# Conditioning products in four column groups, and the context down projection and half of the block product's operands kept in the up pass, in a two-layer DiT block

## The chip, the cores and the metric

One Trainium2 chip, one core. The metric is the device time of one launch in microseconds; three runs of the kernel before gave 3122.32, 3124.87 and 3125.19, median 3124.87. Times below are of one profiled execution of the same program. Engines: TensorE (PE, its weight loads PEld), VectorE (DVE), ScalarE (ACT), GpSimd (POOL) and SyncE (SP), the last two here mostly issuing DMAs.

## The reference

Two layers over a latent of 1024 tokens and a context of 256, width 1024, all fp32. Each layer: a mixer (three token mixers, not touched here), then a gated feed-forward. Conditioning vectors `c`, `c_ctx` give per layer six modulation vectors of 1024:

```
mod   = silu(c)     @ ada_w[layer] + ada_b[layer]      # 1024 -> 6144
mod_c = silu(c_ctx) @ ada_w[layer] + ada_b[layer]
def conv_ffn(h, w_up, conv_w, conv_b, w_down):
    u = dwconv(h @ w_up, conv_w, 1) + conv_b           # 1024 -> 2 x 2816
    gate, val = split(u, 2)
    return (silu(gate) * val) @ w_down                 # 2816 -> 1024
x     = x     + g2  * conv_ffn(modulate(x, ...), ...)
h_ctx = h_ctx + g2c * conv_ffn(modulate(h_ctx, ...), ...)   # layer 0 only
```

## The kernel before, in words

The program is written with symbolic tiles; a scheduler then lays out each engine's instructions in one fixed order and adds the semaphores. It goes by the order of the source, and moves an instruction ahead where its own model of the chip holds it ready. Slots of four tags serve nearly all of SBUF: `L` ("h4", 36 slots of 128x1024), `H2` ("h2", 8 of 128x512), `X` ("h1", 12 of 128x256) and the weight tiles `wh`, `wl` (two each) and `wr`, `wd` (one each). In PSUM tag "a" has two tiles of two banks (`ps`), tag "b" four of one bank (`pb1`).

fp32 products are made of three products of rounded operands: `split` (L313 to 316) writes a rounded copy (ScalarE, L315) and the rest (VectorE, L316), and each product is high x high, high x low, low x high.

**Conditioning**, `ada_gen` (L183 to 214): for each layer and each of three parts of 2048 columns 16 steps. A step loads 128 rows by 1024 columns of `ada_w` (tile `aw`), and multiplies them with `cl`, 32 columns of which two are the conditioning vectors (L199). With only 32 columns a product fills a quarter of the array's columns; `tile_position` names the quarter, and the output stands in the same 32 partitions of PSUM. In step i the two halves of 512 columns go to the quarters 2(i % 2) and 2(i % 2) + 1. The generator is stepped from other code: at the start, in the mixers, and with `ada_load` and `ada_mm` once in each call of `up`.

**Up pass**, `ffn_up` (L1189 to 1247): for f = 0 to 21 and for gate and value (`up`) 48 products of 512 columns into `pu` (latent, two banks), in layer 0 24 of 256 columns into `puc` (context), then the three-tap convolution on ScalarE (L1225) and VectorE (L1226, 1227), Silu on the gate, and gate times value (L1236). The latent's result goes to DRAM in four quarters `actp`, by half of f (11 each) and half of the tokens; the context's stays in `actc`.

**Context down projection**, `ctx_down` (L1250 to 1270), layer 0 only: behind the pass, 22 row blocks of `w_down` (`dr`) are loaded, split, and multiplied into eight blocks of `pd` that stay open over all of f; 528 products of 256 columns, and eight additions into `xc`.

**Block product**, `lat_down` (L1272 to 1432): the latent's product with `w_down` as a two-by-two block product with seven products in place of eight (Winograd's form). Each of the seven stages goes over six `PAIRS` of row blocks, makes the weight operand A from `raw` tiles and the activation operand B from `b` tiles (L1290 loads them back from `actp`), splits both and does 24 products of 512 columns per pair; stages with `isy` = 0 add into `px`, the others into `py`. `finish` adds a stage's result into the residual (L1401), and `fins` holds the steps of the next norm or of the last norm, one of which is done behind each pair from the third on.

Of the kernel before, what the change touches and what calls it, by code (L numbers as in the profile page):

```python
# [9 lines left out]
F32 = mybir.dt.float32  # L10
# [8 lines left out]
P = 128  # L19
D = 1024  # L20
KT = 8
# [66 lines left out]
def tile_dit(ctx: ExitStack, tc: tile.TileContext, x, c, ctxt, c_ctx, ada_w, ada_b, norm_mix_g, norm_ffn_g,  # L88
# [94 lines left out]
    def ada_gen(l, t, al, order=None):  # L183
# [23 lines left out]
        for q4 in range(4):  # L207
            PE.transpose(out=pt[:, q4 * P:(q4 + 1) * P], in_=ev[:, q4 * P:(q4 + 1) * P], identity=ident)
        src = pt.rearrange("p (q j r) -> p j q r", q=4, j=4)[:, :, :, 0:2]
        b = rows["ada_b"][:, l * 48 + t * 16:l * 48 + t * 16 + 16]  # L210
        m_ = mod[l][:, t * 16:(t + 1) * 16, :].rearrange("p (j q) s -> p j q s", j=4)
        V.tensor_tensor(out=m_, in0=src,
                        in1=b.rearrange("p (j q) -> p j q", j=4).unsqueeze(3).to_broadcast([P, 4, 4, 2]), op=add)
# [930 lines left out]
    def project_out(l, y, xl, xc):  # L1144
# [18 lines left out]
        for part in range(2):  # L1163
            for m in range(KT):
# [17 lines left out]

    FH = NF // 2
    PAIRS = [(2 * j, 2) for j in range(FH // 2)] + [(FH - 1, 1)]

    actp = [[[[dp.tile([P, n, 512], F32, name=f"act{l}{a}{b}{j}") for j, (_, n) in enumerate(PAIRS)] for b in range(2)]
             for a in range(2)] for l in range(DEPTH)]

    def ffn_up(l, h, hc_, last=False):  # L1189

        WU = ffn_w_up[l]
        u_, actc = {}, []
# [6 lines left out]
        yield "ready"  # L1199

        def up(f, val):
# [7 lines left out]
            for s_, hh, n in jobs:  # L1209
# [3 lines left out]
                if s_:  # L1213
                    if val:
                        u = H2("uc")[:, 0:C]
                    else:
                        if f % 4 == 0:
                            actc.append(L("actc"))
                        u = actc[-1][:, (f % 4) * C:(f % 4 + 1) * C]
                        u_[1, f] = u  # L1220
                else:
                    u = L("u")
                    if not val:
                        u_[0, f] = u
# [3 lines left out]
                if not val:  # L1228
                    with sact if last and f == NF - 1 else ExitStack():
                        S.activation(out=u, in_=u, func=AF.Silu)  # L1230
                        if last and f == NF - 1:
                            S.preload_act_table_set(LN_EXP)
                else:
                    g = u_.pop((s_, f))
                    o = g if s_ else u
# [320 lines left out]
```

## Time and profile before

| what | value |
|---|---|
| runs, median | 3124.87 us |
| profiled execution, its own time | 3125.18 us |
| its span, first to last instruction | 3123.4 us |
| PE, DVE, ACT, POOL busy | 2971.0, 1742.1, 1313.2, 168.4 us |
| mean granted TensorE clock | 0.98 |
| moved by DMA | 329.93 MB |

The span is what the views of the trace cover; the time of a run is 1.8 us longer. An engine's busy time is no limit by itself: only the chain of waits tells which engine the end waited for. A row of a timeline names the engine, the line, the operation, what it writes and reads, how many are merged in it, and in brackets how long its engine had been idle and what ended that.

### The profile page before, as it was taken

The page shows a single profiled execution, that of the slowest core. Times are in us where ns is not written, and L with a number is a line of the kernel's source. Part 1 is how long each engine was busy: PE and PEld are TensorE (multiplying, and loading weights), DVE is VectorE, ACT ScalarE, POOL GpSimd, SP SyncE. Part 2 cuts the span into 40 slices and gives each one's busy share as a digit, 9 for nine tenths or more (in the row PEclk, how much of TensorE's full clock was granted, in tenths as well). Part 3 has the DMA queues.
Part 4 walks back from the last instruction along what each step waited for, and adds up shares of the span by engine and source line. Part 5 has one row for each costly group of instructions (what it writes and reads, how often), then busy time and mean ns, then how long its engine had stood idle before and what let it go on. Part 6 is the DMA issues. An engine that isn't in the chain of part 4 may idle for free.

```text
span 3123.4 us, 40811 instructions
## 1 busy us (share of the span) xinstructions
PE 2971.0 (95%) x16088; PEld 2325.1 (74%) x16088; DVE 1742.1 (56%) x2639; ACT 1313.2 (42%) x2219; POOL 168.4 (5%) x265
## 2 busy tenths in 40 slices
PE   6999898999999999999899899998999999999998
PEld 4867565558888888888877687776678888887776
DVE  5466555665633333334677656767746333334885
ACT  5365663673422222223334445785744222223333
POOL 1000002000000000000000000002000000000000
PEclk8999899999999999999999899999999999999998
DMA  7212146414222232113864310024044222223842
GB/s 288 67 49 61 54 133 166 135 56 149 93 88 88 86 97 88 48 61 119 285 200 145 96 29 21 25 71 106 10 154 144 72 76 68 75 74 122 295 148 83
DMA packets 273952, 329.93 MB, mean 106 GB/s; under 512 B 18620, under 2 KB 200032, under 8 KB 273760
## 3 DMA queue, kind: packets, MB, share of 16 engines
q1 hardware_dynamic: 249840, 254.36, 26.3%
q0 software_dynamic: 23744, 72.89, 6.7%
q8 instruction: 127, 2.08, 0.3%
q14 instruction: 65, 0.53, 0.1%
q10 hardware_dynamic: 176, 0.07, 0.0%
HBM read 268.00 MB, written 59.24 MB: 105 GB/s over the span
## 4 chain that ended last, share of the span: by engine, by line
PE 83%; ACT 6%; DVE 5%; DMA 4%; issue 2%; SPq 0%; ACTq 0%; DVEq 0%; POOLq 0%
PE pu L341 31%; PE pl L341 9%; PE px L1422 7%; PE py L1422 5%; PE puc L341 4%; PE ada L199 3%; PE iv L587 3%; PE sc L1005 3%; PE yo L1160 3%; PE yo L1154 2%; PE pov L1047 2%; PE pt L1030 2%; PE pc L341 2%; PE hd L668 2%; PE pg L833 1%
## 5 line engine op out<-in xcount | busy, mean ns | idle before, releaser
L341 PE MATMUL pu<-hh,wh 128*128 128x512 f32 x1408 | 554.4, 394 | 2.0 <-ACT u L1225 1.3
L341 PE MATMUL pu<-hh,wl 128*128 128x512 f32 x1408 | 553.1, 393 | 0.0
L341 PE MATMUL pu<-hl,wh 128*128 128x512 f32 x1408 | 549.8, 391 | 0.0
L315 ACT CAST wh<-wr 128x1024 fp32r<-128x1024 f32 x154 | 161.3, 1049 | 516.6 <-PE pu L341 277.5
L316 DVE TENSOR_TENSOR wl<-wr,wh 128x1024 fp32r<-128x1024 f32 x154 | 188.6, 1225 | 339.7 <-ACT wh L315 332.8
L341 PEld LDWEIGHTS pu<-hh,wh 128*128 128x128 f32 x1408 | 264.4, 188 | 81.0 <-issue 22.9
L341 PEld LDWEIGHTS pu<-hl,wh 128*128 128x128 f32 x1408 | 264.4, 188 | 58.8 <-issue 0.5
L341 PEld LDWEIGHTS pu<-hh,wl 128*128 128x128 f32 x1408 | 264.5, 188 | 58.2 <-issue 1.1
L1226 DVE SCALAR_TENSOR_TENSOR u<-pu,col_fcb,u 128x1023 f32<-128x1023 f32 x44 | 56.4, 1283 | 379.5 <-ACT u L1225 379.4
L1225 ACT ACTIVATE u<-pu,col_nf,col_fcw 128x1024 f32<-128x1024 f32 x44 | 53.1, 1206 | 385.2 <-PE pu L341 385.2
L341 PE MATMUL pl<-hh,wh 128*128 128x512 f32 x512 | 210.2, 410 | 1.7 <-ACT K L616 0.7
L341 PE MATMUL pl<-hh,wl 128*128 128x512 f32 x512 | 205.9, 402 | 0.5 <-DVE wl L316 0.5
L341 PE MATMUL pl<-hl,wh 128*128 128x512 f32 x512 | 203.8, 398 | 0.0
L315 ACT CAST ah<-raw 128x512 fp32r<-128x512 f32 x132 | 76.4, 618 | 209.0 <-PE px L1422 92.0
L341 PEld LDWEIGHTS pl<-hh,wh 128*128 128x128 f32 x512 | 96.2, 188 | 39.5 <-issue 18.5
L1011 DVE TENSOR_REDUCE st<-sc 128x1 f32<-128x641 f32 (+2 forms) x144 | 106.8, 745 | 26.2 <-ACT sc L1010 24.6
L316 DVE TENSOR_TENSOR al<-raw,ah 128x512 fp32r<-128x512 f32 x132 | 86.1, 687 | 55.4 <-ACT ah L315 50.7
L341 PEld LDWEIGHTS pl<-hh,wl 128*128 128x128 f32 x512 | 96.2, 188 | 26.3 <-issue 5.5
L1014 ACT ACTIVATE pb<-sc,st 128x641 f32<-128x641 f32 (+2 forms) x144 | 106.3, 739 | 20.2 <-DVE st L1011 17.3
L1227 DVE SCALAR_TENSOR_TENSOR u<-pu,col_fcw,u 128x1023 f32<-128x1023 f32 x88 | 112.8, 1282 | 3.0
L341 PEld LDWEIGHTS pl<-hl,wh 128*128 128x128 f32 x512 | 96.2, 188 | 23.5 <-issue 5.5
L1005 PEld LDWEIGHTS sc<-kc,qt 128*128 128x128 f32 x288 | 44.2, 192 | 88.3 <-ACT pb L1014 36.5
(415 smaller groups left out, 6580.1 us busy)
## 6 DMA issues: line engine op xcount, KB each, us to landing
raw<-in_ffn_w_down_dram SPq DMA_DIRECT2D x220, 256.0 KB
aw<-in_ada_w_dram SPq DMA_DIRECT2D x96, 512.0 KB
wr<-in_ffn_w_up_dram SPq DMA_DIRECT2D x88, 512.0 KB
act<-u POOLq DMA_DIRECT2D x88, 256.0 KB, 3.0
b<-act SPq DMA_DIRECT2D x40, 512.0 KB
wr<-in_w_in_dram SPq DMA_DIRECT2D x34, 512.0 KB
wr<-in_w_out_dram SPq DMA_DIRECT2D x128, 128.0 KB
dr<-in_ffn_w_down_dram SPq DMA_DIRECT2D x22, 512.0 KB
```

The source lines that it names most:

```text
L199: PE.matmul(out=pt[32 * q:32 * q + 32, 0:512], lhsT=cl[:, k, :], rhs=wr[:, j * 512:(j + 1) * 512], start=(k == 0), stop=(k == KT - 1), til ...
L315: S.copy(out=hi, in_=raw)
L316: eng.tensor_tensor(out=lo, in0=raw, in1=hi.bitcast(F32), op=sub)
L341: PE.matmul(out=o, lhsT=wl[k] if pi == 2 else wh[k], rhs=hl[k] if pi == 1 else hh[k], start=(k == 0 and pi == 0), stop=(k == nk - 1 and pi ...
L587: PE.matmul(out=po[:, 0:384], lhsT=hh[1 if pi == 1 else 0][k][:, t0:t0 + P], rhs=wiv[k][1 if pi == 2 else 0], start=(k == 0 and pi == 0), ...
L668: PE.matmul(out=pv[64 * hf:64 * hf + 64, ci, :].rearrange("p (h t) -> p h t", h=2), lhsT=kw(ci, hf), rhs=z[:, :, b:b + 64], start=True, st ...
L1005: PE.matmul(out=o_, lhsT=qt[:, hh, :], rhs=k_[:, ksl], start=(pi == 0), stop=(pi == 1 and not ms))
L1011: V.tensor_reduce(out=st[:, 0, c_], in_=sc[:, s0:769], axis=mybir.AxisListType.X, op=ALU.min)
L1014: S.activation(out=pb, in_=sc[:, s0:769], func=AF.Exp, bias=st[:, 0, c_], scale=-1.0, accum_out=st[:, 1, c_])
L1160: PE.matmul(out=o, lhsT=wl[k] if pi == 2 else wh[k], rhs=a[1 if pi == 1 else 0][:, s_], start=False, stop=(ki == 3 and pi == 2), skip_grou ...
L1227: V.scalar_tensor_tensor(out=u[:, 0:n - 1], in0=pu[:, 1:n], scalar=cw(2), in1=u[:, 0:n - 1], op0=mult, op1=add)
L1422: PE.matmul(out=acc[m], lhsT=(al if pi == 2 else ah)[:, i, c_], rhs=(bl if pi == 1 else bh)[:, i, :], start=((isy or si == 0) and j == 0 a ...
```

## The change

1. `ada_gen`: a step's 1024 columns go as four products of 256 columns to the four quarters; even and odd steps write the two halves of the bank.
2. `ffn_up` now takes f in halves by its parity. The first half of the tokens of the even f (in layer 1 of the odd f too) stays on chip as `bt[a, 0, j]`; the rest goes to DRAM (`park`), and where b11 - b01 is needed that difference is formed here and parked in place of b01.
3. In layer 0 `ctx_act` loads and splits the row block of `w_down` for each f, and `ctx_down` does the products of every two f, four tiles of two blocks, behind the next gate's `puc`; each tile is added into `xc` at once (88 additions in place of 8).
4. `lat_down`: operands are made one pair ahead of the products (`operands`); `b` tiles that are still loaded are loaded from POOL's queue; the fifth stage's A is summed by a DMA that adds (`accum_op=add`).

```diff
@@ ada_gen
-            for j in range(2):
-                q = 2 * (i % 2) + j
-                PE.matmul(out=pt[32 * q:32 * q + 32, 0:512], lhsT=cl[:, k, :], rhs=wr[:, j * 512:(j + 1) * 512],
-                          start=(k == 0), stop=(k == KT - 1), tile_position=(0, 32 * q))
+            h0 = i % 2 * 256
+            for q in range(4):
+                PE.matmul(out=pt[32 * q:32 * q + 32, h0:h0 + 256], lhsT=cl[:, k, :], rhs=wr[:, q * 256:(q + 1) * 256],
+                          start=(i == 0), stop=(i == 2 * KT - 1), tile_position=(0, 32 * q), skip_group_check=True)
@@ ffn_up
+        def lat_act(f, g, u):
+            fh, k = f % 2, f // 2
+            j, i = k // 2, k % 2
+            if fh == 0 or hc_ is None:
+                if i == 0:
+                    b_tile(fh, j)
+                for b, o in ((0, bt[fh, 0, j][:, i, :]), (1, u[:, 512:1024])):
+                    V.tensor_tensor(out=o, in0=g[:, b * 512:b * 512 + 512], in1=u[:, b * 512:b * 512 + 512], op=mult)
+            else:
+                V.tensor_tensor(out=u, in0=g, in1=u, op=mult)
+                G.dma_start(out=park[l][1, 0, j][:, i, :], in_=u[:, 0:512])
+            if fh == 0:
+                even.append(u)
+                return
+            e = even.pop()
+            G.dma_start(out=park[l][1, 1, j][:, i, :], in_=u[:, 512:1024])
+            V.tensor_tensor(out=e[:, 512:1024], in0=u[:, 512:1024], in1=e[:, 512:1024], op=sub)
+            G.dma_start(out=park[l][0, 1, j][:, i, :], in_=e[:, 512:1024])
+        def ctx_act(f, a):
+            dr = L("dr")
+            nc.sync.dma_start(out=dr, in_=WD[f * P:(f + 1) * P, :])
+            dh, dl = L("dh", F32R), L("dl", F32R)
+            split(dh, dl, dr)
+            ac = H2("ac", F32R)
+            ah, al = ac[:, 0:C], ac[:, C:2 * C]
+            split(ah, al, a)
+            grp.append((dh, dl, ah, al))
+            if f % 2:
+                g_ = list(grp)
+                grp.clear()
+                cq.extend((g_, m) for m in range(0, KT, 2))
+        def ctx_down(g_, m):
+            pd = pb1("pd")
+            for i, (dh, dl, ah, al) in enumerate(g_):
+                for m_ in range(2):
+                    c_ = slice((m + m_) * P, (m + m_ + 1) * P)
+                    for pi in range(3):
+                        PE.matmul(out=pd[:, m_ * C:(m_ + 1) * C], lhsT=(dl if pi == 2 else dh)[:, c_],
...
+            for m_ in range(2):
+                V.scalar_tensor_tensor(out=xc[m + m_], in0=pd[:, m_ * C:(m_ + 1) * C], scalar=mod[l][:, 40 + m + m_, 1:2],
+                                       in1=xc[m + m_], op0=mult, op1=add)
...
+            if not val:
+                while cq:
+                    ctx_down(*cq.pop(0))
             ada_mm()
@@ lat_down
-            nc.sync.dma_start(out=bt[a, b, j], in_=actp[l][a][b][j])
+            G.dma_start(out=bt[a, b, j], in_=park[l][a, b, j])
...
         def a_p5(j):
-            a11 = raw_a(0, 0, j)
-            for i, x_ in enumerate(a11):
-                tt(x_, x_, s2[j][:, i, :], add)
-            return a11
+            k = PAIRS[j][0]
+            s1 = raw_a(1, 0, j)
+            for i, t_ in enumerate(s1):
+                G.dma_start(out=t_, in_=WD[1, :, k + i, 512:1024], accum_op=add)
+            return s1
...
         def b_p2(j):
-            load_b(1, 0, j)
-            load_b(0, 1, j)
-            load_b(1, 1, j)
-            tt(bt[0, 1, j], bt[1, 1, j], bt[0, 1, j], sub)
             tt(bt[0, 0, j], bt[0, 0, j], bt[0, 1, j], add)
             return bt[1, 0, j]
...
+        todo = [(si, j) for si in range(7) for j in range(len(PAIRS))]
+        ops = [operands(*todo[0])]
+        for q, (si, j) in enumerate(todo):
...
+            if q + 1 < len(todo):
+                ops.append(operands(*todo[q + 1]))
+            ah, al, bh, bl = ops.pop(0)
...
             if j == 1:
                 finish()
             if j > 1 and fins:
                 fins.pop(0)()
@@ the program
-            ctx_down(l, actc, xc)
```

Three places show how the instructions stand. TensorE in the up pass of layer 0, where a call of `up` ends (first before, then now; `puc` is the context's up product, `hh`, `hl` and `wh` the operands of the next call):

```order
L341 MATMUL puc<-ch,wh 128x256
L341 MATMUL puc<-cl,wh 128x256
L341 MATMUL puc<-ch,wl 128x256
L199 MATMUL ada<-aw,cl 32x512 x2
L341 MATMUL pu<-hh_6101,wh 128x512
L341 MATMUL pu<-hl_6109,wh 128x512
```

```order
L1253 MATMUL pd<-ac,dh 128x256 x2
L1253 MATMUL pd<-ac,dl 128x256
L199 MATMUL ada<-aw,cl 32x256 x4
L341 MATMUL pu<-hh_6229,wh 128x512
L341 MATMUL pu<-hl_6237,wh 128x512
L1253 MATMUL pd<-ac,dh 128x256 x2
L1253 MATMUL pd<-ac,dl 128x256
```

Behind every second gate's `puc` now stand 24 products of pd, the conditioning step with its four products, two products of the next call, and the other 24 of pd, where one step alone stood before.

VectorE at the end of the up pass of layer 0, now (`uc` is the last context tile, `dl` and `ac` the last operands of the down projection, `al` and `bd` those of the block product's first pair):

```order
L1276 SCALAR_TENSOR_TENSOR uc<-puc,col_fcb_995,uc 128x255
L1222 TENSOR_TENSOR u<-u 128x1024
L1277 SCALAR_TENSOR_TENSOR uc<-puc,col_fcw_1002,uc 128x255
L1229 TENSOR_TENSOR u<-u 128x512
L1285 TENSOR_TENSOR uc<-uc 128x256
L316 TENSOR_TENSOR dl<-dr,dh 128x1024
L316 TENSOR_TENSOR ac<-uc,ac 128x256
L1257 SCALAR_TENSOR_TENSOR xc_6213<-pd,mod_90,xc_6213 128x256
...
L1257 SCALAR_TENSOR_TENSOR xc_6220<-pd,mod_90,xc_6220 128x256
L316 TENSOR_TENSOR al<-raw,ah 128x512 x2
L316 TENSOR_TENSOR bd<-b,br 128x1024
```

The last group's operands stand behind the latent's two operations, and the first operands of the block product behind all eight additions into `xc`.

ScalarE in the last stage of the block product of layer 0, at the norm of the next layer (`pm` is the sum over the width, `rs` its inverse root, `ah` and `rb`/`br` the rounded operands of a pair; first before, then now):

```order
L235 ACT_TABLE_LOAD
L315 CAST ah<-raw 128x512 x2
L315 CAST rb<-b 128x1024
L236 ACTIVATE rs<-pm,epsc 128x512
L237 ACTIVATE rs<-rs 128x512
L238 ACTIVATE r_13830<-rs 128x512
L286 ACTIVATE hh_13744<-hm,mod_91 128x512
L315 CAST ah<-raw 128x512
```

```order
L264 ACTIVATE sq<-xb 128x512 x3
L315 CAST ah<-raw 128x512 x2
L264 ACTIVATE sq<-xb 128x512 x3
L235 ACT_TABLE_LOAD
L315 CAST ah<-raw 128x512 x2
L315 CAST rb<-b 128x1024
L236 ACTIVATE rs<-pm,epsc 128x512
L237 ACTIVATE rs<-rs 128x512
L238 ACTIVATE r_14169<-rs 128x512
```

The casts in front of `rs` are now those of the pair behind the one that TensorE works on when `rs` is due; the casts behind `rs` belong to the pair after that.

## Rows read from the trace of the kernel before

**Rows 1.** The page, part 4: shares of the chain that ended last.
```profile
PE 83%; ACT 6%; DVE 5%; DMA 4%; issue 2%; SPq 0%; ACTq 0%; DVEq 0%; POOLq 0%
```
**Rows 2.** Stages: length, then busy us of PE, PEld, DVE, ACT, POOL; clock, DMA.
```profile
215.00:526.00 311.00, 292.51 (x1739) 203.72 (x1737) 174.15 (x287) 173.76 (x291) 22.18 (x22) 0.97 0.32 92
...
822.00:1240.00 418.00, 416.35 (x2109) 333.35 (x2105) 165.37 (x203) 108.31 (x139) 13.95 (x26) 1.00 0.28 85
...
1459.00:1546.00 87.00, 75.06 (x560) 71.36 (x558) 57.66 (x73) 39.82 (x56) 1.11 (x2) 0.94 0.79 274
1546.00:1774.00 228.00, 217.05 (x922) 175.01 (x921) 170.02 (x232) 84.27 (x122) 10.85 (x18) 0.98 0.44 145
```
**Rows 3.** The chain in order of time: start us, us, what.
```profile
879.87 11.20 PE pu L341 x48
...
894.88 11.20 PE pu L341 x48
...
1255.04 11.00 PE pu L341 x48
1266.04 2.83 PE puc L341 x24
...
1448.62 11.00 PE pu L341 x48
...
1546.09 29.37 PE px L1422 x127
...
1628.00 6.73 DMA raw<-in_ffn_w_down_dram
```
**Rows 4.** TensorE in order of time, at the start and in the up pass.
```profile
33.76 7.18 PE L199 MATMUL ada<-aw,cl 128*32 128x512 f32 x52
...
893.83 1.05 PE L199 MATMUL ada<-aw,cl 128*32 128x512 f32 x4
```
**Rows 5.** TensorE's weight loads in order of time, at the start.
```profile
38.21 0.12 PEld L199 LDWEIGHTS ada<-aw,cl 128*32 128x32 f32 x4 [0.31 <-issue]
38.64 0.12 PEld L199 LDWEIGHTS ada<-aw,cl 128*32 128x32 f32 x4 [0.31 <-issue]
```
**Rows 6.** Stages, line 199 alone: length, PE and PEld.
```profile
822.00:1240.00 418.00, 29.58 (x112) 4.02 (x108) 1.00 0.28 85
```
**Rows 7.** VectorE in order of time, end of the up pass of layer 0.
```profile
1462.21 1.28 DVE L1227 SCALAR_TENSOR_TENSOR u<-pu,col_fcw,u 128x1023 f32<-128x1023 f32 x1
...
1464.58 1.22 DVE L1236 TENSOR_TENSOR u<-u 128x1024 f32<-128x1024 f32 x1
1465.72 0.48 DVE L1226 SCALAR_TENSOR_TENSOR uc<-puc,col_fcb,uc 128x255 f32<-128x255 f32 x1
...
1467.17 0.42 DVE L1236 TENSOR_TENSOR actc<-actc,uc 128x256 f32<-128x256 f32 x1
```
**Rows 8.** TensorE in order of time, context down projection.
```profile
1469.52 0.63 PE L1265 MATMUL pd<-ac,dh 128*128 128x256 f32 x2
...
1470.16 0.63 PE L1265 MATMUL pd<-ac,dh 128*128 128x256 f32 x2
...
1473.12 0.40 PE L1265 MATMUL pd<-ac,dh 128*128 128x256 f32 x2
1473.47 0.40 PE L1265 MATMUL pd<-ac,dh 128*128 128x256 f32 x2
```
**Rows 9.** TensorE in order of time, block product of layer 0: two waits.
```profile
1643.85 0.51 PE L1422 MATMUL py<-bd,ah 128*128 128x512 f32 x1 [2.21 <-DVE bd L316]
...
1757.74 0.80 PE L1422 MATMUL px<-rb,ah 128*128 128x512 f32 x1 [6.07 <-ACT ah L315]
```
**Rows 10.** ScalarE and VectorE in order of time, before the second of these.
```profile
1751.71 0.69 ACT L236 ACTIVATE rs<-pm,epsc 128x512 f32<-128x512 f32 x1 [5.32 <-PE pm L270]
...
1756.33 1.29 DVE L1304 TENSOR_TENSOR raw<-raw,s 128x512 f32<-128x512 f32 x2
```
**Rows 11.** All engines in order of time, start of layer 1's block product.
```profile
2867.91 1.20 ACT L1225 ACTIVATE u<-pu,col_fcb,col_fcw 128x1024 f32<-128x1024 f32 x1
...
2874.18 1.22 PE L1422 MATMUL px<-br,ah 128*128 128x512 f32 x2 [6.59 <-ACT br L315]
```
**Rows 12.** The page, part 6: DMA issues.
```profile
act<-u POOLq DMA_DIRECT2D x88, 256.0 KB, 3.0
```

More of the change, by code (lines that the diff above doesn't have):

```diff
@@ L208, in ada_gen @@
             PE.transpose(out=pt[:, q4 * P:(q4 + 1) * P], in_=ev[:, q4 * P:(q4 + 1) * P], identity=ident)
[L209 to L213, printed above, removed]
+        src = pt.rearrange("p (h b q r) -> p h b q r", h=2, b=2, q=4)
+        b_ = rows["ada_b"][:, l * 48 + t * 16:l * 48 + t * 16 + 16].rearrange("p (h q b) -> p h b q", h=2, q=4)
+        m_ = mod[l][:, t * 16:(t + 1) * 16, :].rearrange("p (h q b) s -> p h b q s", h=2, q=4)
+        for h in range(2):
+            V.tensor_tensor(out=m_[:, h], in0=src[:, h, :, :, 0:2], in1=b_[:, h].unsqueeze(3).to_broadcast([P, 2, 4, 2]), op=add)
         yield "end"
@@ L1184, in tile_dit, with two, ffn_up @@
     PAIRS = [(2 * j, 2) for j in range(FH // 2)] + [(FH - 1, 1)]
[L1186 to L1192, printed above, removed]
+    park = [{(a, b, j): dp.tile([P, n, 512], F32, name=f"act{l}{a}{b}{j}") for j, (_, n) in enumerate(PAIRS)
+             for a, b in ((0, 1), (1, 0), (1, 1))} for l in range(DEPTH)]
+    def two(t_):
+        return t_.rearrange("p (a t) -> p a t", a=2)
+    def ffn_up(l, h, hc_, xc, bt, last=False):
+        WU, WD = ffn_w_up[l], ffn_w_down[l]
+        u_, odd, even, grp, cq = {}, {}, [], [], []
         jobs = [(0, h, T)] + ([(1, hc_, C)] if hc_ is not None else [])
@@ new lines, in operands @@
+        def operands(si, j):
+            n = PAIRS[j][1]
+            a, b = stages[si][0](j), stages[si][1](j)
+            ah, al = two(wtile("wh", "ah", F32R)), two(wtile("wl", "al", F32R))
+            bh, bl = (two(wtile(t_, t_[1:] + "b", F32R, 1) if j % 2 else L("b" + t_[1:], F32R)) for t_ in ("wr", "wd"))
+            if isinstance(a, list):
+                for i in range(n):
+                    split(ah[:, i, :], al[:, i, :], a[i])
+            else:
+                split(ah[:, 0:n, :], al[:, 0:n, :], a[:, 0:n, :])
+            split(bh[:, 0:n, :], bl[:, 0:n, :], b)
+            return ah, al, bh, bl
@@ new lines, in lat_down @@
+        todo = [(si, j) for si in range(7) for j in range(len(PAIRS))]
+        ops = [operands(*todo[0])]
+        for q, (si, j) in enumerate(todo):
+            n, isy = PAIRS[j][1], stages[si][2]
+            if j == 0:
+                acc = [pb1("py") for _ in range(4)] if isy else X
+                if si in (0, 2, 3, 5):
+                    load_x(*{0: (0, 0), 2: (1, 0), 3: (1, 1), 5: (0, 1)}[si])
+            if q + 1 < len(todo):
+                ops.append(operands(*todo[q + 1]))
+            ah, al, bh, bl = ops.pop(0)
+            for m in range(4):
+                c_ = slice(m * P, (m + 1) * P)
+                for i in range(n):
+                    for pi in range(3):
+                        PE.matmul(out=acc[m], lhsT=(al if pi == 2 else ah)[:, i, c_], rhs=(bl if pi == 1 else bh)[:, i, :],
+                                  start=((isy or si == 0) and j == 0 and i == 0 and pi == 0),
+                                  stop=(j == len(PAIRS) - 1 and i == n - 1 and pi == 2), skip_group_check=True)
+            if j == 1:
+                finish()
+            if j > 1 and fins:
+                fins.pop(0)()
+            if j == len(PAIRS) - 1:
+                ends.append((si, acc, stages[si][3]))
```

117 lines of the change are left out of this document (35 added, 82 removed).

## The prediction

> **What bounds the kernel now.** I read the chain of waits first: 83% of the span on it is TensorE [rows 1]. So a change pays where it shortens TensorE's own work or an idle stretch of TensorE. The stage table says where these lie [rows 2]: the up pass of layer 0 is full (416.35 us busy in its first 418), while the context down projection keeps TensorE busy 75.06 of 87 us, the block product of layer 0 217.05 of 228. The reader is to see that the change touches these stages and, with the conditioning, a stretch of the mixers before them that is busy 292.51 of 311. The profiled execution took 3125.18 us, 0.3 above the median of the runs; sums are made against it.
>
> **Conditioning products.** In the up pass a call of `up` lasts 15.01 us with a step of `ada_gen` (879.87 to 894.88) and 13.83 without (11.00 + 2.83 from 1255.04) [rows 3], so a step costs 1.18. Its two products of 512 columns run side by side, as four records within 1.05 us [rows 4]. At the start 13 steps stand in a row (x52 in 7.18 us [rows 4]), and there the weights of one step come 0.43 us after those of the last [rows 5]: neighbouring steps write other column groups, so four products share the array and a step's work is done in half the time of a lone one (0.86). The change gives each step all four groups with 256 columns each. A lone step should fall by 0.43; the 13 in a row stay. The other 0.3 of the 1.18 (emptying and refilling the array) stays. Bounds: no gain, if TensorE is held up by issuing 8 products and 8 weight loads for 4 and 4; 0.59, half of 1.18, if that 0.3 shrinks as well. I take 0.43, since [rows 5] shows four streams at full pace.
>
> The Trainium skill, "TensorE: Matmul & The Clock Gate", section "Part 3: Packing small matmuls — row/col tiling", measured 3.07 times for four tiles of rows, not 4, and column tiles close to that model; by it a lone step would gain an estimated 0.30 (1.71 us of work in 0.56, where two groups need 0.86), in all some 9 us less. The pace of [rows 5] does not bear it out here.
>
> Of 96 steps (2 layers, 3 parts, 16 each) 13 stand in a row; 28 of the 83 lone ones lie in the up pass (x112, four records each [rows 6]), where TensorE has no gaps: 28 x 0.43 = 12.0 us. The other 55 lie before it; there TensorE idles some 6% [rows 2] and waits at times for the step's weights, so I count 80%: 55 x 0.43 x 0.8 = 19. **Sum 31.**
>
> **Context down projection.** Now: the last `puc` ends at 1462.45 (1448.62 + 11.00 + 2.83) and the block product starts at 1546.09 [rows 3], 83.6 us. Its 528 products take the pace of `puc`, 24 in 2.83 us [rows 3]: 62.3. They move into the pass, 48 for every two f, behind `puc` of the next f. Between groups I cost the waits low: pd takes one of four banks, two are held by `ada` and `puc`, so the third pd waits until VectorE has read `puc`. VectorE is free 1.0 us after `puc` ends (1462.21 + 1.28) and does `wl`, one operation of `puc`, one of pd and the second of `puc`: 1.0 + 1.22 + 3 x 0.48 = 3.7 us [rows 7]; a bank of pd is free 0.5 later. Two pd (2.8) and the step (0.75) take TensorE 3.6. I put 0.3 us on each of ten groups, 3 us, on the debit side. The cover is VectorE's free half; if it goes, this is rival B. The `dr` loads join SP's queue ahead of `wr`; a `wr` load has about 9 us to spare of each 13.8.
>
> The last group has no cover. `dl` and `ac` of f = 21 are made behind the latent's work: from 1.0 us after `puc` VectorE does 0.48 + 1.22 + 0.48 + 0.61 (half the width of 1.22) + 0.42 + 1.22 + 0.42 = 4.9 us [rows 7], so TensorE, with 0.7 us of f = 20 to do, stands 5.2. In the old kernel the products behind such a pause came three in 0.64 us, later three in 0.35 [rows 8], from 1466.58 to 1472.5: its lower clock (1.2 for 2.4 GHz). 28 of the remaining 42 would cost 0.095 more, 2.7. Then, by VectorE's order, `al` and `bd` of the first block product stand behind the last two additions into `xc`: 0.96 + 1.29 + 1.22 = 3.5 us. So 62.3 + 11.4 = 73.7 against 83.6: **10.** Bounds: 21 with no stall, 0 if the stalls double.
>
> **Block product, layer 0.** 924 products at 0.229 us (48 in 11.00 [rows 3]) are 212; it takes 228 [rows 2]. Of its waits 2.21 us lie behind its third product and 6.07 near its end [rows 9]. The last has one cause: ScalarE does `rs` (Ln, Exp, Square) at 1751.71, and the casts and subtractions of the next operands stand behind it (1756.33) [rows 10]. With operands one pair ahead, the casts of that pair stand before `rs`, and TensorE has 5.5 us of products for a chain of about 8: 2.5 left, and with it goes half of the lower clock that follows. Gain 5. Up to the third product VectorE drops one addition per pair (b11 - b01 is formed in the pass), and one in the fifth (DMA does it); raw loads and slots are the same. I count the wait of 2.21 as gone, 2. **Sum 7;** bounds 0 and 13.
>
> **Block product, layer 1.** Its first operand is now on chip, but little follows. TensorE stood 6.59 us until 2874.18 [rows 11], put down to the cast of a tile that DMA brings. The new order puts that cast and `bd` behind the last `u` anyway: ScalarE's 1.2, then on VectorE 1.28 + 0.6 + 1.28 + 1.29 + 1.22, some 6.9 us after the last product, against 7.5 (2867.9 to 2875.4, where its first two products end). So 0.6, by the same reasons as in layer 0 some 2.5 in the middle, and 1 at the end: **4;** bounds -3 and 12.
>
> **New and unpriced.** 22 DMAs from POOL add into a loaded tile. The nearest rows are plain POOL transfers, median 3.0 us to landing for the `act` stores, and a `raw` load of 6.73 [rows 3, 12]. One that must read, add and write could take twice the last, 13. Eight `raw` slots at two per 5.5 us give 22 us from load to reuse, so even that hides if transfers overlap: 0, other end rival C. POOL also takes over the `b` loads, 33 pieces of 256 KB in layer 0 and 22 in layer 1; most are asked for a whole product, 30 us, before their use.
>
> Total 31 + 10 + 7 + 4 - 3 = 49: **3076 us.** The measurement tells 0.2%, 6 us, from no change.
>
> **Rivals.** A: four groups gain nothing (issue-bound). For it: twice the instructions; against: the pace at the start. 3076 + 31 = 3107. B: VectorE, with some 4 us more work per f (`dl` 1.22, `ac` 0.42, four of pd 1.92, the subtraction), comes 2 us late at each group and TensorE waits for banks: 11 x 2 = 22, 3098. For it: VectorE takes its work in order, and `puc` stands behind `wl`; against: it is busy 165 of 418 us [rows 2]. D: the ends are covered better than I read (no 11.4, middle waits gone): -20, 3056. C, the other side: the adding DMAs go one after another. The fifth product has 11 and lasts 30.3 us; at t each it lasts 11 t, twice. 49 us are lost at t = 5.0, and from 5.3 the kernel is slower by 0.2%; at 6.73 it costs 2 x (74 - 30) = 87, 3163. For it: each waits for its load and POOL issues in order, with other transfers between; against: [rows 12], where stores of one size follow each other and land in 3.0 us.
>
> The Trainium skill, "SBUF — State Buffer", section "Who interferes with whom", says that transfers issued by GpSimd can be starved while VectorE holds shared ports; that would feed C, and the 88 stores of [rows 12] beside a working VectorE show no such thing.
>
> **How the numbers follow.** Forecast 0.55, A 0.10, B 0.14, D 0.13, C 0.08. The forecast's own bounds reach from about 3050 to 3100. The range takes in A, B and D: 3046 to 3112; C is left out. Faster by over 0.2%: all but C and a tail of A and B with both, 0.88; within: 0.05; slower: 0.07.
>
> **What would show it.** A lone step: about 0.75 us more than a call without one, in place of 1.18. pd inside the pass at 0.118 each, and nothing of L1253 idle but the last group, some 5 us before and 3 after it. The wait before `px` in the last product of layer 0 at 2 to 3 us. The start of layer 1's block product unchanged within a microsecond. Wrong if `ada` records still fill 1 us a step, if pd idles at every group, or if the fifth product waits for `raw`.

## The result, and the profile after

The changed kernel takes 3073.16 us (median of four runs, 3071.11 to 3081.94) against 3125.03 of the kernel before: ratio 0.9841, 95% interval 0.9821 to 0.9861. The forecast was 3076. The profiled execution spans 3069.0 us, 54.4 less than before. Busy times and the chain of waits, from the page:

```profile
PE 2925.5 (95%) x16472; PEld 2323.1 (76%) x16472; DVE 1764.7 (57%) x2746; ACT 1312.6 (43%) x2219; POOL 184.6 (6%) x284
PE 82%; ACT 6%; DVE 6%; DMA 4%; issue 2%; SPq 0%; ACTq 0%; DVEq 0%; POOLq 0%
```

TensorE is busy 45.5 us less, and the chain is made as before [rows 1]. The total says little about the terms, so both kernels are cut at the same marks on TensorE's timeline: the first product of `pu`, the last of `puc`, the last `px` of a layer, and so on.

| stretch, us | before | changed | gain |
|---|---|---|---|
| start to the first `pu` of layer 0 | 815.1 | 789.8 | 25.3 |
| to the last `puc` | 647.4 | 691.2 | -43.8 |
| to the first `px` that others follow at once (1544.6; 1493.0) | 82.2 | 12.1 | 70.1 |
| to the end of the block product of layer 0 | 229.7 | 226.1 | 3.6 |
| to the first `pu` of layer 1 (norm, mixer) | 604.9 | 608.9 | -4.0 |
| up pass of layer 1 | 488.4 | 488.6 | -0.2 |
| its block product, from the last `pu` | 235.8 | 231.7 | 4.1 |
| final norm | 20.0 | 20.7 | -0.7 |

How far single executions of the same instructions differ is seen where two programs share a stretch and the order of its instructions on TensorE, VectorE and ScalarE: run 1 repeats the old block products, run 2 the changed ones. Layer 0: 229.7 and 230.2, 226.1 and 225.5. Layer 1: 235.8 and 233.0, 231.7 and 233.4. So the gain in layer 0 is clear of this spread, and the 4.1 in layer 1 is not: the repeats alone would give -0.4.

**Conditioning.** The chain in order of time in the up pass, in calls with a step and, later, without:

```profile
1016.56 11.20 PE pu L341 x48
1027.76 2.72 PE puc L341 x24
1030.48 0.57 PE ada L199 x8
1031.05 11.20 PE pu L341 x48
...
1271.74 10.99 PE pu L341 x48
1282.73 2.72 PE puc L341 x24
1285.45 10.99 PE pu L341 x48
```

A step now takes 0.57 us and a call with one 14.49, 0.78 more than the 13.71 of a call without, where it was 15.01 against 13.83 [rows 3]. The 0.2 us that the first products behind a step lose (11.20 for 10.99) is still there.

**End of the pass.** TensorE, with the first and the last products of the final group and the block product's first:

```profile
1480.75 0.40 PE L1253 MATMUL pd<-ac,dh 128*128 128x256 f32 x2
...
1482.79 0.28 PE L1253 MATMUL pd<-ac,dl 128*128 128x256 f32 x1
1484.14 0.35 PE L1253 MATMUL pd<-ac,dh 128*128 128x256 f32 x1 [1.07 <-DVE uc L1277]
...
1485.42 0.74 PE L1253 MATMUL pd<-ac,dh 128*128 128x256 f32 x4 [0.33 <-ACT ac L315]
1486.45 0.38 PE L1253 MATMUL pd<-ac,dh 128*128 128x256 f32 x1 [0.29 <-DVE ac L316]
...
1488.82 0.28 PE L1253 MATMUL pd<-ac,dl 128*128 128x256 f32 x1
1488.94 0.62 PE L1457 MATMUL px<-br,ah 128*128 128x512 f32 x2
1492.97 0.80 PE L1457 MATMUL px<-bd,ah 128*128 128x512 f32 x1 [3.40 <-DVE bd L316]
```

Eighteen products of the last group (1480.75 to 1482.79, x2 and x1 six times) need only f = 20 and run while VectorE makes `dl` and `ac`; 1.7 us of stalls stay, and none of these products of pd runs at the lower clock (0.12 us each). Then VectorE does what the 3.40 us wait for, first the eight additions into `xc`, then the operands:

```profile
1487.35 3.23 DVE L1257 SCALAR_TENSOR_TENSOR xc<-pd,mod,xc 128x256 f32<-128x256 f32 x8 [0.95 <-PE pd L1253]
1490.49 1.29 DVE L316 TENSOR_TENSOR al<-raw,ah 128x512 fp32r<-128x512 f32 x2
1491.69 1.22 DVE L316 TENSOR_TENSOR bd<-b,br 128x1024 fp32r<-128x1024 f32 x1
```

**Block product, layer 0.** The waits that answer to [rows 9], two in the third product, one early in the fourth, one in the last (rows between them left out):

```profile
1557.14 0.50 PE L1457 MATMUL px<-br,al 128*128 128x512 f32 x1 [1.80 <-DVE al L316]
...
1576.83 0.50 PE L1457 MATMUL px<-db,ah 128*128 128x512 f32 x1 [1.58 <-DVE db L316]
...
1594.59 0.50 PE L1457 MATMUL py<-br,al 128*128 128x512 f32 x1 [2.84 <-DVE al L316]
...
1710.24 0.50 PE L1457 MATMUL px<-br,ah 128*128 128x512 f32 x1 [0.62 <-ACT ah L315]
```

The wait of 6.07 us behind the norm is 0.62, while around the third product 6.7 us stand (with 0.44 at 1588.50) for the 4.8 of before (2.35, 0.25, 2.21); the same instructions had 5.8 in run 1 and 7.3 in run 2. ScalarE shows why the former went: the cast of the pair that TensorE takes next now stands ahead of `rs`.

```profile
1698.65 1.04 ACT L315 CAST rb<-b 128x1024 fp32r<-128x1024 f32 x1
1704.21 0.69 ACT L236 ACTIVATE rs<-pm,epsc 128x512 f32<-128x512 f32 x1 [4.51 <-PE pm L270]
```

By stages (length, then PE, PEld, DVE, ACT, POOL, clock, DMA share, GB/s), first, third, fourth and fifth product:

```profile
1493.00:1524.60 31.60, 31.60 (x131) 25.78 (x132) 24.64 (x29) 10.76 (x16) 6.63 (x12) 0.95 0.87 328
1556.00:1592.00 36.00, 32.59 (x132) 25.71 (x132) 27.69 (x34) 10.81 (x14) 5.78 (x10) 0.95 0.81 286
1592.00:1626.20 34.20, 31.61 (x131) 25.80 (x132) 27.68 (x37) 13.81 (x20) 9.01 (x11) 0.95 0.78 207
1626.20:1656.50 30.30, 30.30 (x134) 24.80 (x133) 21.17 (x28) 12.67 (x19) 2.66 (x4) 1.00 0.59 160
```

The first has no gap but a clock of 0.95, since it begins at the lower clock behind the wait of 3.40 us (0.43 us from one product of 512 columns to the next at 1493.56). The fifth, for which the 11 adding DMAs work, is without a gap at 30.3 us. They land in about the time of the plain load of 6.73 in [rows 3] (the median from issue to landing is last):

```profile
raw<-in_ffn_w_down_dram POOLq DMA_DIRECT2D x11, 256.0 KB, 6.8
```

**Block product, layer 1**, its start, which answers to [rows 11]:

```profile
2819.59 0.50 PE L1457 MATMUL px<-br,ah 128*128 128x512 f32 x1 [3.03 <-ACT br L315]
2821.35 0.77 PE L1457 MATMUL px<-br,ah 128*128 128x512 f32 x1 [1.25 <-DVE u L1277]
2823.72 0.79 PE L1457 MATMUL px<-bd,ah 128*128 128x512 f32 x1 [1.61 <-DVE bd L316]
```

The third product starts 7.15 us behind the last `pu` (2816.57); before it was 7.84 (2867.59 to 2875.43).

### The profile page after: what moved, and what is told of

It reads as the page before. It is cut to its first block, busy times and chain, and to the rows that moved or that the text cites. A ratio compares the mean times of both kernels' runs of the same rounds, so it can differ in the third digit from the quotient of the medians.

```text
span 3069.0 us, 41616 instructions
## 1 busy us (share of the span) xinstructions
PE 2925.5 (95%) x16472; PEld 2323.1 (76%) x16472; DVE 1764.7 (57%) x2746; ACT 1312.6 (43%) x2219; POOL 184.6 (6%) x284
## 4 chain that ended last, share of the span: by engine, by line
PE 82%; ACT 6%; DVE 6%; DMA 4%; issue 2%; SPq 0%; ACTq 0%; DVEq 0%; POOLq 0%
PE pu L341 31%; PE pl L341 9%; PE px L1457 7%; PE py L1457 4%; PE puc L341 4%; PE iv L587 3%; PE yo L1160 3%; PE sc L1005 3%; PE yo L1154 2%; PE pov L1047 2%; PE pc L341 2%; PE pt L1030 2%; PE pd L1253 2%; PE ada L199 2%; PE hd L668 2%
## 5 line engine op out<-in xcount | busy, mean ns | idle before, releaser
L341 PEld LDWEIGHTS pu<-hh,wh 128*128 128x128 f32 x1408 | 264.5, 188 | 66.9 <-issue 11.4
```

Of the source, the lines that this page charges most:

```text
L341: PE.matmul(out=o, lhsT=wl[k] if pi == 2 else wh[k], rhs=hl[k] if pi == 1 else hh[k], start=(k == 0 and pi == 0), stop=(k == nk - 1 and pi ...
```

## The experiments

Each ratio is to the kernel before, run on the same chip.

**1. The conditioning step alone.** The kernel before with

```diff
-            for j in range(2):
-                q = 2 * (i % 2) + j
-                PE.matmul(out=pt[32 * q:32 * q + 32, 0:512], ..., rhs=wr[:, j * 512:(j + 1) * 512], ...)
+            h0 = i % 2 * 256
+            for q in range(4):
+                PE.matmul(out=pt[32 * q:32 * q + 32, h0:h0 + 256], ..., rhs=wr[:, q * 256:(q + 1) * 256], ...)
```

> The kernel before with the new conditioning step alone. If the four column groups are worth what the two traces show (25.7 us ahead of the up pass, and 28 steps at 0.39 in it), 3125 - 37 = 3088, with the up pass beginning near 797 and the block product of layer 0 beginning 83 to 84 us behind the last context product, as before. If part of the 25.7 comes from the rest of the change (another order of the scheduler), the up pass begins later than 800 and the time is nearer to the forecast's 31, that is 3094. If TensorE were bound by the issue of the products (rival A), 3125.

3087.3 us, ratio 0.9894 (0.9879 to 0.9909). The up pass begins at 791.1, 24.0 us earlier than before, and is 13.4 us shorter (634.0 for 647.4). The other stretches are as before within 0.6 us, except that the block product of layer 1 is 2.8 shorter, with the same instructions in the same order. So 37 us of the gain are the step's own by the stretches; the interval of the ratio says 28 to 38. Over all programs here the up pass begins at 813.5 to 815.1 with the old step and at 787.9 to 791.1 with the new one (the 25.7 us of the expectation are 25.3 by the table's marks). A call with a step lasts 14.60 us (1174.25 to 1188.85) for 15.01, 0.41 less, and 28 of them give 11.5.

```profile
1174.25 11.20 PE pu L341 x48
1185.45 2.83 PE puc L341 x24
1188.28 0.57 PE ada L199 x8
```

**2. Everything but the conditioning step.** The changed kernel with the lines of run 1 turned back.

> The changed kernel with the old conditioning step. If the parts add, 3073 + 37 = 3110: up pass beginning near 822, context products still inside the pass, the block product 12 us behind the last context product. If the parts share a gain (the longer step hides the waits of the context products), less than 37 is lost: below 3106.

3113.97 us, ratio 0.9975 (0.9966 to 0.9984). This is neither of the two: the parts do not only add, they help each other. By spans the step alone gives 39.0 (3084.4), the rest alone 11.0 (3112.4), both 54.4. The chain shows where the rest loses:

```profile
1227.42 2.88 PE pd L1253 x24
1230.30 0.98 PE ada L199 x2
1231.28 3.07 PE pd L1253 x24
1234.35 0.97 PE ada L199 x2
```

In five of the eleven groups of pd the scheduler puts the two old products of a step at two places, and each half costs 0.97 to 0.98 us by itself, as much as the whole step where its products stand together. The up pass is 708.9 us, 61.5 longer than before, where the same groups add 57.1 with the new step (691.2 against 634.0 of run 1): 4.3 of the 4.4 us that the parts lack by spans.

**3. VectorE's addition in place of the adding DMA.**

```diff
-            s1 = raw_a(1, 0, j)
-            for i, t_ in enumerate(s1):
-                G.dma_start(out=t_, in_=WD[1, :, k + i, 512:1024], accum_op=add)
-            return s1
+            a11 = raw_a(0, 0, j)
+            for i, x_ in enumerate(a11):
+                tt(x_, x_, s2[j][:, i, :], add)
+            return a11
```

> The changed kernel with the sum of the fifth product's weight operand by VectorE from a loaded block and the kept s2, as before, in place of the adding DMA. Forecast: the DMA is hidden and VectorE has time in that stage, so the same within 2 us. Rival: the adding DMAs, which run beside the loads of the third and fourth product, delay those loads; then the waits of the third product (1.80, 1.58, 0.44, 2.84 us in layer 0) shrink and the kernel is 2 to 5 us faster. Rival C as forecast (they go one after another): tens of us faster, which the fifth product without any wait speaks against already.

3070.4 us, ratio 0.9841 (0.9826 to 0.9855), span 3068.4: the same. The block products are 1.3 and 0.4 us shorter, and the waits around the third product only change places (4.58 us at one of them). That the adding DMAs gain or cost anything is not shown.

**4. Operands not one pair ahead.**

```diff
-            if q + 1 < len(todo):
-                ops.append(operands(*todo[q + 1]))
-            ah, al, bh, bl = ops.pop(0)
+            ah, al, bh, bl = ops.pop(0) if q == 0 else operands(si, j)
```

> The changed kernel with the operands of a pair made just before its products, as before, not one pair ahead. If one pair ahead removed the wait behind the norm (6.07 to 0.62 us in the last product of layer 0), that wait comes back and with it some lower clock: 5 to 7 us slower, 3079. If working ahead also moved the vector work of the third product and made its waits longer (6.66 against 4.81 us in layer 0), those fall by 2 per layer and the sum is only 1 to 3 us slower, 3075.

3088.56 us, ratio 0.9889 (0.9867 to 0.9911), span 3085.1: 16 us longer than the changed kernel, more than either theory. The block products grow by 7.8 and 7.3 us. In layer 0 the wait behind the norm is back and one in the third product is longer:

```profile
1578.89 0.79 PE L1455 MATMUL px<-db,ah 128*128 128x512 f32 x1 [4.85 <-DVE db L316]
...
1710.47 0.80 PE L1455 MATMUL px<-rb,ah 128*128 128x512 f32 x1 [6.06 <-ACT ah L315]
```

**5. One pair ahead alone.** The kernel before, with the loop of the changed one in `lat_down` (`operands` for pair q + 1 ahead of the products of pair q).

> The kernel before, with nothing but the operands of the block products one pair ahead. In the changed kernel this is worth 8 us in layer 0 and 7 in layer 1 (its absence cost that much). If it is worth the same by itself, the block products take 222 and 222 us in place of 229.7 and 229.2, and the kernel 3122 - 15 = 3107; then the other parts of the change cost 8 us in layer 0 and 4 in layer 1. If its worth depends on them (operands kept on chip, fewer vector operations), it is the forecast's 7 + 4 or less, 3111 to 3118.

3111.36 us, ratio 0.9965 (0.995 to 0.9979). The block product of layer 0 takes 221.7 us for 229.7, that of layer 1 227.0 for 235.8 from the last `pu`: it is worth 8.0 and 8.8 us by itself. But 5.4 are lost between the layers (610.3 for 604.9). Part of the 8 us is the clock. The last product of layer 0, before and in this run:

```profile
1734.30:1774.40 40.10, 33.97 (x134) 26.17 (x133) 28.78 (x44) 18.39 (x28) 2.46 (x5) 0.91 0.18 59
```

```profile
1731.00:1764.00 33.00, 32.34 (x138) 25.26 (x136) 25.78 (x39) 18.00 (x28) 2.46 (x5) 1.00 0.16 56
```

With the wait of 6.07 went the products at the lower clock behind it. From product to product the last takes 40.2 us before and 32.4 here (the second window begins 0.6 us early), so nearly all of the 8.0 is gained there. In layer 1 the third product starts 5.8 us behind the last `pu` here, for 7.84 before and 7.15 in the changed kernel. It also follows that the other edits cost the block products 4.4 us in layer 0 (226.1 against 221.7) and 4.7 in layer 1 (231.7 against 227.0). Run 4 against the kernel before says the same without operands one pair ahead: 4.2 in layer 0 (233.9 against 229.7), 3.2 in layer 1 (239.0 against 235.8).

Where it lies is seen product by product. The last of the seven takes 32.4 to 33.0 us in this run and the changed kernel, in both layers, and 35.4 to 40.8 in the kernel before, run 1 and run 4. The third and the fourth together take in layer 0 67.8 before, 68.6 in run 1 and 67.8 in run 5, against 71.3 in the changed kernel, 70.7 in run 2 and 70.8 in run 4. So of the 4.4 us 3.5 lie there, and 0.8 in the first (31.5 from 1492.97 on, for 30.7), behind the wait of 3.40 us. The next runs ask which edit costs the 3.5.

**6. b11 later.**

```diff
         def b_p7(j):
-            load_b(1, 1, j)
             return bt[0, 1, j]
...
         def b_p5(j):
+            load_b(1, 1, j)
             tt(bt[0, 0, j], bt[1, 1, j], bt[0, 0, j], sub)
```

> The changed kernel with the load of b11 asked for in the fifth product, where it is first used, not in the fourth. In the changed kernel five of these 512 KB loads fall in the third product, in which DMA engines are busy 0.81 of the time and VectorE waits for raw tiles. If they are what makes the third product wait (6.7 us at four places in layer 0, 4.81 before), those waits fall by 2 or more and the kernel is 2 to 4 us faster, 3070. Rival: the third product is bound by its own six loads a pair and by the eight slots of raw tiles: same within 1 us.

3081.62 us, ratio 0.9868 (0.9854 to 0.9883): slower than the changed kernel by 11.7 us of span, though the intervals overlap a little, and neither theory has it. The waits of the third product fall only from 6.7 to 5.2 in layer 0, and a new one stands near the end of the fourth, in both layers; the third and the fourth together take 76.0 us there, 4.7 more:

```profile
1626.01 0.80 PE L1457 MATMUL py<-db,ah 128*128 128x512 f32 x1 [4.42 <-DVE db L316]
...
2961.91 0.50 PE L1457 MATMUL py<-db,ah 128*128 128x512 f32 x1 [4.90 <-DVE db L316]
```

**7. A11 - A21 kept.** Run 6, and the difference of the third product kept for the fourth.

```diff
-            s3 = a_s3(j)
+            a11, a21 = raw_a(0, 0, j), raw_a(1, 0, j)
             a22 = raw_a(1, 1, j)
-            t_ = two(L("s2"))
+            t_, d_ = two(L("s2")), two(L("s3"))
...
-            for i, (x_, y_) in enumerate(zip(a22, s3)):
-                tt(t_[:, i, :], x_, y_, sub)
+            for i, (x_, y_, z_) in enumerate(zip(a22, a11, a21)):
+                tt(d_[:, i, :], y_, z_, sub)
+                tt(t_[:, i, :], x_, d_[:, i, :], sub)
```

> The changed kernel with the difference A11 - A21 of the third product kept in six more tiles and used again in the fourth, where it was loaded (22 blocks a layer) and subtracted (11 operations) a second time; b11 is then loaded in the fifth product, as in the run before. The fourth product's loads go, 5.8 MB a layer, and so does the wait at its start (2.84 us in layer 0, 1.42 in layer 1), since its operands need no DMA. Expected 4 to 6 us faster over both layers, 3068. Rival: the six tiles are taken from the slots that b tiles and residual blocks wait for, and what is gained there is lost in waits for slots: same or slower.

3063.34 us, ratio 0.9809 (0.9794 to 0.9824; the intervals just touch), span 3061.3, 7.7 below the changed kernel. The third and the fourth product of layer 0 together take 65.1 us for 71.3. Of the waits around the third one is left in each layer, at its start:

```profile
1559.66 0.50 PE L1456 MATMUL px<-br,al 128*128 128x512 f32 x1 [2.69 <-DVE al L316]
...
2885.18 0.80 PE L1456 MATMUL px<-br,al 128*128 128x512 f32 x1 [2.53 <-DVE al L316]
```

**8. And the single weight slots for even pairs.** `F32R, 1) if j % 2 else` becomes `F32R, 1) if j % 2 == 0 else`.

> The run before, with the rounded B operands of even pairs, not of odd ones, in the two single weight slots. In the changed kernel the first pair's B takes two of the 36 tiles, and its cast stands behind the last activation of the up pass in layer 1 (3.03 + 1.25 + 1.61 us of waits before the second product). If a free tile is what it waits for, the cast goes ahead of the last call and these waits fall to about 1 us, 4 to 5 us faster than the run before. The end of layer 0's block product frees both weight slots one pair earlier, so the wait of 8.4 us for the next layer's first weights should fall by up to 2.7. Rival: the cast is late because the scheduler's model puts it there for another reason: no change at either place.

3066.14 us, ratio 0.9822 (0.9808 to 0.9837): not faster than run 7. The wait for the next layer's first weights falls from 9.03 us in run 7 to 2.50, but the second one there grows from 0.63 to 3.28. A new wait stands early in the first product, and a longer one early in the third, where a short pair (n = 1) may leave the slot too late:

```profile
1504.24 0.50 PE L1456 MATMUL px<-db,ah 128*128 128x512 f32 x1 [2.34 <-DVE db L316]
...
1558.57 0.80 PE L1456 MATMUL px<-db,ah 128*128 128x512 f32 x1 [4.16 <-DVE db L316]
```

That the short pair is the reason was argued from the order of the slots, not tested. In layer 1 the three waits are 2.02, 2.95 and 1.10 within its first 13 us, no less than before.

**9. b11 earlier.** `load_b(1, 1, j)` moves from `b_p7` to the head of `b_p2`.

> The changed kernel with the load of b11 asked for in the second product, as in the kernel before, not in the fourth. The kernel before with operands one pair ahead needs 221.7 us for the block product of layer 0 and the changed kernel 226.1 from its second product of 512 columns on, 4.4 more, most of it in the third product. If the five b11 loads inside the third product are that difference, waits there fall from 6.7 to 5.3 us in layer 0 and the kernel is 3 to 6 us faster, 3068. Rival: it comes from POOL's queue, which carries the b loads, or from the adding DMAs (1.7 us over both layers in the run without them): same within 1 us.

3070.08 us, ratio 0.9829 (0.9815 to 0.9844), span 3068.5. The time is the same within the intervals. Waits around the third product fall to 5.3 us as forecast and each block product is 2.4 us shorter; 4.3 us are lost in other stretches. In layer 0, where the spread between like executions is 0.6, b11 is part of the 4.4 us, not all of it.

**10. b tiles from SP's queue.** In `load_b`, `G.dma_start` becomes `nc.sync.dma_start`.

> The changed kernel with the b tiles loaded from SP's queue, as before, not from POOL's. If the order of issue on POOL, where a b load stands behind adding DMAs and stores that wait, delays the third product, its waits fall to the 5.3 us of the kernel before with operands one pair ahead, 2 to 4 us faster. Rival: on SP a b load that waits for a free tile holds up the raw loads behind it, which is why they were moved: third product worse, 2 to 5 us slower.

3064.36 us, ratio 0.9815 (0.98 to 0.9829), span 3068.0. The block products are 1.7 and 4.3 us shorter. The medians say 9 us faster than the changed kernel, the spans of the two profiled executions 1.0; the intervals just touch, so a gain is likely but not shown.

**11. The first pair earlier.** Run 7, with `lat_down` begun from inside the up pass, so that `operands(0, 0)` stands ahead of the last additions into `xc` in layer 0, and ahead of the last call's activation in layer 1:

```diff
                 u = H2("uc")[:, 0:C] if s_ else L("u")
+                if last and f == NF - 1 and val:
+                    tail()
...
             up(f, 1)
+        if not last:
+            tail()
         while cq:
```

> The run that keeps A11 - A21, with the first pair of the block product made earlier: in layer 0 ahead of the last additions into xc, in layer 1 ahead of the last activation of the up pass. If only the order of VectorE and ScalarE delays that pair, the wait of 3.40 us in layer 0 falls below 1 and the three waits in layer 1 (3.03, 1.16, 1.60) below 2 together, and with them goes some lower clock: 7 to 9 us faster than the run before, 3055. Rival: another wait takes their place, since the last additions or the second pair then come later: 0 to 3 us faster.

3054.39 us, ratio 0.9776 (0.976 to 0.9793), span 3055.3, 6.0 below run 7. In layer 0 the wait of 3.40 is 0.29; in layer 1 the waits are gone at the start, two of 1.43 and 0.53 us stand 12 us later:

```profile
2823.57 0.73 PE L1461 MATMUL px<-br,ah 128*128 128x512 f32 x2 [1.43 <-ACT br L315]
2824.83 0.50 PE L1461 MATMUL px<-bd,ah 128*128 128x512 f32 x1 [0.53 <-DVE bd L316]
```

**12. Runs 10 and 11 together.**

> The run before, with the b tiles loaded from SP's queue. In the changed kernel this took 1.7 us off the block product of layer 0 and 4.3 off that of layer 1, and the span fell by 1.0 only. If the gain belongs to the third product (its waits 5.1 us in layer 0 in place of 6.7, and in layer 1 2.1 in place of 4.9), little of it is left here, since with A11 - A21 kept the third product's end no longer waits: same within 3 us, 3054. If SP's queue is better in general, 4 us faster, 3050; if b11, which waits for a tile that the fourth product frees, holds up the raw loads of the fifth behind it, a new wait at the fifth product and 2 to 5 us slower.

3046.78 us, ratio 0.9749 (0.973 to 0.9768), span 3047.0: the fastest of all, 75.6 us below the kernel before on its chip (3122.39). By the medians it beats run 11 by 7.6 us, more than any theory had, but the intervals overlap. The block product of layer 1, run 11 and this one:

```profile
2811.00:3034.40 223.40, 218.65 (x951) 178.07 (x950) 157.95 (x209) 83.46 (x124) 21.80 (x31) 0.98 0.49 155
```

```profile
2809.00:3026.00 217.00, 214.95 (x951) 175.86 (x950) 157.58 (x209) 83.54 (x124) 15.92 (x20) 1.00 0.51 159
```

Of the 6.4 us 2.7 are waits (1.43, 0.53 and 2.80 became one of 2.05), the rest the lower clock behind them.

## Why the prediction was right

The forecast's five terms sum to 49 us, the stretches above to 54. The sign and the size were right, and so were the mechanisms of the two large terms and of the wait at the norm. The terms themselves were off in both directions, so that the total comes this close is in part luck. Of the signs set down, the step's cost, the pace of pd and the start of layer 1's block product came as said; the stall before the last group (1.7 us for some 5) and the wait behind the norm (0.62 for 2 to 3) came out smaller.

**Conditioning, 31: measured 37** (24.0 + 13.4, run 1). The step was right: 0.43 forecast and 0.41 measured, and of a step's cost 0.78 is left where 0.75 was forecast. What failed is the 80% for steps ahead of the up pass. TensorE's idle time there did not take any of the gain: idle until the first `pu` is 61.8 us before and 63.0 in run 1 (791.1 less 728.13 busy), and the 55 lone steps give 23.3, 0.42 each; the other 0.7 come from the 13 in a row (6.53 us for 7.18), which were forecast to stay. The estimate of 0.30 a step by the figure of the Trainium skill, "TensorE: Matmul & The Clock Gate", section "Part 3: Packing small matmuls — row/col tiling", which would have given some 9 us less, is not borne out here. Rival A (no gain, issue-bound) is out.

**Context down projection, 10: measured 13.0** (82.2 less 12.1 behind the last `puc` and 57.1 inside the pass; no run moves it alone). The forecast took 83.6 for the 82.2, since it read the start of the block product off a row of the chain (1546.09), where the timeline has the first `px` at 1544.62. The products take 5.76 us for 48, 0.120 each for the 0.118 forecast. The step that failed is "TensorE, with 0.7 us of f = 20 to do, stands 5.2": the schedule runs 18 products of f = 20 in three banks, 2.1 us, and TensorE stood 1.7, without the lower clock that I had counted with 2.7. That clock can come, though: in run 11 the same three stalls are followed by products of pd 0.21 us apart (1484.60 to 1487.37, granted clock 0.51, the lower of the two levels), here 0.12. The 3.5 us for the block product's first operands were right (3.40), and run 11 shows their cause, the order on VectorE.

**Bank waits, -3: none.** Inside the pass not one product of pd has idle time before it in the changed kernel. Rival B is out. With the old step five groups do pay some 1 us each (run 2), for another reason: the scheduler takes a step apart.

**Block product of layer 0, 7: measured 3.6**, the 8.0 of run 5 less 4.4. The 5 at the norm were undersized: the last product takes 7.7 us less (40.2 to 32.5), for the wait fell to 0.62, not 2.5, and all of its lower clock went. The 2 at the third product had the wrong sign: the third and the fourth together take 3.5 us more. "Raw loads and slots are the same" left out that the b loads were moved in time and to another queue. As single reversals, which overlap, an earlier b11 gives back 2.4 us of the block product (run 9) and SP's queue 1.7 (run 10); the 1.3 without adding DMAs (run 3) are little more than the 0.6 by which like executions differ. That b01 and, in layer 0, b10 are now loaded in the first product, and that tiles kept from the up pass hold slots, was not reversed, so which edit costs most stays open. The last 0.8 us lie in the first product, at the lower clock behind the 3.40 us of the context's last group.

**Block product of layer 1, 4: measured 4.1**, a difference of the same two: 8.8 gained by one pair ahead (run 5), 4.7 lost by the rest. That the number agrees is luck. The repeats in runs 1 and 2 would make it -0.4, and the parts were otherwise than forecast. The middle (third and fourth product) gained nothing (69.1 us for 68.6) where 2.5 was forecast. The end gained 4.0 (33.0 for 37.0) where 1 was forecast: two waits of 1.35 and 0.53 us behind the final norm's steps went, with the lower clock behind them. The start was forecast within a microsecond (0.6 gained, 0.7 measured); the forecast's 7.5 us before ran from ScalarE's operation at 2867.91, not from the last `pu`. That its first operand is on chip is not what helps there: in run 5, which loads it, the third product starts 1.3 us sooner still.

**Rival C** is out: the 11 adding DMAs of layer 0 are issued between 1608.4 and 1634.2 us and land in 6.8 us (median), several at a time, and the fifth product has no wait. Rival D was the nearest: its missing waits at the end of the pass (over half of its 11.4) and behind the norm are real, but the third and fourth product and the next layer took that back.

**Not forecast, 4 us lost between the layers.** Half of it stands in the first products of layer 1's mixer, where casts of the weights `ivh` stand apart on ScalarE, between the norm's steps:

```profile
1726.61 0.83 ACT L315 CAST ivh<-ivr 128x768 fp32r<-128x768 f32 x1 [3.99 <-DMA ivr<-in_w_in_dram]
1727.35 0.72 ACT L286 ACTIVATE hh<-hm,mod 128x512 fp32r<-128x512 f32 x1
1727.97 1.13 ACT L264 ACTIVATE sq<-xb 128x512 f32<-128x512 f32 x2
...
1730.14 0.81 ACT L315 CAST ivh<-ivr 128x768 fp32r<-128x768 f32 x1
```

From the last `px` of layer 0 to the mixer's `hd` 99.4 us pass, 97.3 before; 99.2 in run 5, which has one pair ahead, 97.5 in run 4, which has not, and 96.9 in run 1. The other runs, all with one pair ahead, have 97.9 to 100.3, except run 8 (96.2), in which the first weights come earlier. So that half goes with one pair ahead. The other half (2 us, and up to 5 in other runs) lies in later parts of the mixer, whose instructions no edit names; what moves them is open.

## What to carry to other kernels

Here work moved onto a full engine cost its own time there and no more (57.1 us for 480 products at 0.12), since what it waits for is made a whole group earlier; the price shows at the last group, where nothing covers it, and there the order on the helping engine decides. Making operands one step ahead of their products was worth more than the stall that it removed (8.0 us for 6.07 in layer 0): in the kernel before, the first eleven products behind that stall start 0.42 to 0.61 us apart, not 0.23. Loads that such a change moves in time or to another queue are terms of the sum of their own: here the other edits took back about half of that gain, a later b11 alone cost another 4.7 us in layer 0, and keeping a difference on chip instead of loading its parts again was worth about 7.7 us. And a stretch read from one execution of each kernel has a spread; a term smaller than that is not measured by it.

## What was not expected of the hardware

- A lone step with four products of 256 columns in four column groups takes 0.57 us, one with two of 512 in two groups 0.98; a single product of 512 alone takes the same 0.98 (run 2). In these three cases the time goes by the columns of one product, not by how many groups work.
- DMAs that add into a loaded tile of 256 KB land in 6.8 us (the median of layer 0's 11), about as the one plain load of that size on the chain (6.73), and they overlap.
- The same b loads from SP's queue in place of POOL's shortened both block products in both pairs of runs: by 1.7 and 4.3 us (10 against the changed kernel) and by 2.3 and 6.4 (12 against 11), where like executions differ by up to 0.6 and 2.8. The Trainium skill, "SBUF — State Buffer", section "Who interferes with whom", says that a DMA held up by VectorE is one that GpSimd issues; whether that or the order of issue on POOL is the reason was not tried.
- The 24 products of `puc` take 2.83 us in the calls of the kernel before from 876 on, all but the last; in the changed one some calls take 2.72 and, from 1269 on, all, at the same clock. In run 1 the first nine full calls take 2.72 and the others up to the last 2.83, so it does not hang on the moved context products; no run says why.
